# Deferred sums, evacuations, key transposes and exponentials, and one feed-forward split issued earlier, in a hybrid decoder layer

## Chip, cores and metric

The kernel runs on one core of one Trainium2 chip. The metric is the time of one execution on the device in microseconds (us); three runs are shown for the kernel before, and one further execution was taken with the hardware profiler.

## What is computed

One decoder layer over 512 tokens of width 1024, in float32. Three token mixers read the same normed input; their outputs are projected, gated, summed and projected again; a SwiGLU feed-forward follows. Both halves are residual.

```python
h = rms_norm(x, g_mix);  proj = h @ w_in             # q,k,v of two mixers, q of the third, three gates
y_m = moba_attention(rope(norm(q_m)), rope(norm(k_m)), v_m)    # 8 heads of 64; at 512 tokens: causal softmax
y_f = fox_attention(norm(q_f), norm(k_f), v_f, log_sigmoid(f_logit + b))   # 8 heads, cumulative bias
mk, mv = split(rms_norm(mem, g_mem) @ w_mem_kv)      # 256 memory tokens, 4 heads of 128
y_c = memory_attention(norm(q_c), norm(mk), mv)
merged = sum(sigmoid(a_i) * (y_i @ w_br_i)); x = x + merged @ w_out
h2 = rms_norm(x, g_ffn); x = x + (silu(h2 @ w_gate) * (h2 @ w_up)) @ w_down
```

## The kernel before

**Arithmetic.** Every float32 operand of a projection is split in two: a rounded high part, copied by ScalarE (`w_hi`, `hT` and so on), and the rest, a subtraction on VectorE (`w_lo`, the second half of `hT`). A product is then three passes on TensorE: high by high, high by low, low by high. Some products (units of the input projection, the gate and up matrices) are done with seven block products instead of eight, which needs sums of operand blocks first; `sums_of_h` makes those of the normed input: eight `whole_h` (one 128x512 addition each), eight `th_sum` (one 128x512 each) and four two-stage splits `th_split`.

**Order.** The order of instructions is written by hand. `mm` issues one matmul and counts estimated time; after each 1,250 ns of that (six matmuls of 512 columns, twelve of 256) it calls `tick` (L278). A tick (1) splits one weight piece ahead (`split_next`: the low part left over from the last tick, then the next high part), (2) runs what `later(n, fn)` has put off by n ticks (`run_due`), (3) takes steps from the list of work beside the matmuls (`side`, filled by `beside`, at a rate per tick), (4) runs what was left in `pend`. `flush_side` empties the list and then runs (2) and (4) twice more without a matmul. Each engine works through its own queue in this order, so an instruction that waits holds up those behind it on its engine.

**First stretch.** `mem_groups` projects the memory tokens, keys first, then values (48 matmuls, eight ticks, each). Beside it run the squares of x, and from the 11th tick on four steps of `turn_x`: each transposes two column blocks of the scaled x, and `evac_split` (L318) takes the bank out, high part on ScalarE, low part on VectorE. `rms_mem` makes the memory tokens' row norms. After `flush_side` come the values' evacuations (`vslots`), the sums of h, and the query projection `head_chunk(NT, 128, ...)`, 96 matmuls or 16 ticks, reading four weight pieces in turn, six matmuls each in the first row of tokens. The memory keys' `head_chunk(MT, 128, ..., lag=22)` has put off its own steps: norm factors on VectorE and ScalarE, a multiplication on POOL per 128 tokens (`norm`, L565), and one step per head at which the keys are transposed (`turn`, L622).

**Attention.** Four lists of 16 units each (two of `moba`, two of `fox`) run beside projections through `attention`: at step n the scores of unit n (L924), its masking and row minimum on VectorE (`softmax`, L935 to L945); the product with the values of a half two steps after its transposes; the transposes of unit n-4 (`turn`, L975, evacuated by `evac_split`); and last the exponential of unit n on ScalarE (`exps`, L953), which puts off by one tick the reciprocal (VectorE, L956) and the multiplication of the row (POOL, L957). The memory attention has a list of its own, which the diff leaves alone.

**Feed-forward start.** The second half of the output projection does four groups of 128 tokens. After the third, `turn2` and `right_split` prepare the first two right-hand operands. After the fourth, the last row norm is made, the put-off work is drained, ScalarE loads the table of silu, and `product` goes through the block products in the order of `FIRST`: (0, M1), (0, M2), (1, M1), (1, M2), ... `split_op(u, m)` (L1250) is the split of a left operand: high part on ScalarE (L1254), low part on VectorE (L1257). That of (1, M1) is issued from the first hooks of the first product.

Of the kernel before, what the change touches and what calls it, by code (L numbers as in the profile page):

```python
# [19 lines left out]
NT = S // P  # L20
M = 256
MT = M // P
D = 1024
KD = D // P
# [18 lines left out]
def hybrid_layer(ctx, tc, rope, x, mem, g_mix, w_in, b_forget, g_q_moba, g_k_moba, g_q_fox,  # L43
# [274 lines left out]
    def later(n, fn):  # L318
        deferred.append([n, fn])


    def evac_split(hi, lo, src, scale=None, late=False):
        if scale is None:
            act.activation(hi, src, AF.Copy)

            def low():
                dve.tensor_tensor(lo, src, f32(hi), op=OP.subtract)
        else:
            act.activation(hi, src, AF.Copy, scale=scale)

            def low():
                dve.scalar_tensor_tensor(lo, src, scale, f32(hi), op0=OP.mult, op1=OP.subtract)
        if late:
            pend.append(low)
        else:
            low()

    def rsqrt(ss, inv_n, w, delay=None, rows=None, nh=1, out=None):

# [90 lines left out]
    gcol = consts.tile([P, NG], F32, name="gcol")  # L430
# [120 lines left out]
    def head_rest(raws, tw, ss, ntok, d, kind, blocks, lag, rows=None, e=2, out=None):  # L551

        nh = tw // d
        w = ntok * nh
        if rows is not None:
            e = lag - 5
        rs = rsqrt(ss[:, :w], 1.0 / d, w, e, rows=rows, nh=nh, out=out)

        def of_tiles(t0, n):
            per = 1024 // tw  # L560
            return raws[t0 // per][:, t0 % per * tw:(t0 % per + n) * tw]

        def norm(t0, n):
            r3 = of_tiles(t0, n).rearrange("p (g d) -> p g d", d=d)
            pool.tensor_tensor(r3, r3, rs[:, t0 * nh:(t0 + n) * nh, None].to_broadcast([P, n * nh, d]),  # L565
                               op=OP.mult)

        def rotate():
            j = 0 if blocks[0][0] == GQM else 1
            r4 = of_tiles(0, ntok).rearrange("p (t h d) -> p t h d", t=ntok, h=nh)  # L570
            tmp = small.tile([P, ntok, nh, 16], F32, name="rtmp", tag="rtmp", bufs=1)
            for a in (0, 8):
                pool.tensor_tensor(
                    tmp[:, :, :, a:a + 8], r4[:, :, :, 8 - a:16 - a],
                    sg[:, j, :, None, a:a + 8].to_broadcast([P, ntok, nh, 8]), op=OP.mult)
            pool.tensor_tensor(r4[:, :, :, :16], r4[:, :, :, :16],
                               cg[:, j, :, None, :].to_broadcast([P, ntok, nh, 16]), op=OP.mult)
            pool.tensor_tensor(r4[:, :, :, :16], r4[:, :, :, :16], tmp, op=OP.add)

        n = 512 // tw  # L580
        for i in range(ntok // n if out is None else 0):
            later(e + 3 + i, lambda i=i: norm(i * n, n))
        if kind == "rope":
            later(e + 5, rotate)

        def turn_pair(blk):
            gc, dst, i, gains = blocks[blk]
            g = gains[:, gc:gc + 1]
            tb = bank("a")
            for tt in range(ntok):  # L590
                pe.transpose(tb[:, tt * P:(tt + 1) * P],  # L591
                             of_tiles(tt, 1)[:, blk * P:(blk + 1) * P], ident)
            if gc in (GQM, GQF):
                o = slot("qT", F32R)
                dst[i] = o
                o2 = [(o[:, 0:512], o[:, 0:512]), (o[:, 512:1024], o[:, 512:1024])]
            else:
                ks = [slot("kT", F32R), slot("kT", F32R)]
                dst[i] = ks
                o2 = [(k[:, 0:512], k[:, 512:1024]) for k in ks]  # L600
            for h, (hi, lo) in enumerate(o2):
                r = slice(64 * h, 64 * h + 64)
                act.activation(hi[r], tb[r], AF.Copy, scale=g[r])
            for h, (hi, lo) in enumerate(o2):
                r = slice(64 * h, 64 * h + 64)
                q = slice(64 - 64 * h, 128 - 64 * h)
                dve.scalar_tensor_tensor(lo[q if gc in (GQM, GQF) else r], tb[r], g[r],
                                         f32(hi[r]), op0=OP.mult, op1=OP.subtract)
            if gc not in (GQM, GQF):
                def double():  # L610
                    nc.gpsimd.dma_start(ks[0][64:128, :1024], ks[0][0:64, :1024])
                    nc.gpsimd.dma_start(ks[1][0:64, :1024], ks[1][64:128, :1024])
                later(1, double)

        def turn(blk):
            if d == 64:
                return turn_pair(blk)
            gc, dst, i, gains = blocks[blk]
            tb = bank("a")
            w = ntok * P  # L620
            for tt in range(ntok):
                pe.transpose(tb[:, tt * P:(tt + 1) * P],  # L622
                             of_tiles(tt, 1)[:, blk * P:(blk + 1) * P], ident)
            o = slot("qkT", F32R)
            evac_split(o[:, :w], o[:, w:2 * w], tb[:, :w], gains[:, gc:gc + 1])
            dst[i] = (o[:, :w], o[:, w:2 * w])
        order = sorted(range(len(blocks)), key=lambda blk: blocks[blk][2])
        for j, blk in enumerate(order):
            later(lag + (j if d == 128 or len(blocks) == 2 else 2 * j), lambda blk=blk: turn(blk))
# [23 lines left out]
        later(2, lambda: scale_x(2 * half))  # L653
        later(2, lambda: scale_x(2 * half + 1))

    def turn_x(k):
        tb = bank("a")
        for t in range(NT):
            pe.transpose(tb[:, t * P:(t + 1) * P], x_t[t][:, k * P:(k + 1) * P], ident)
        o = slot("hT", F32R)  # L660
        evac_split(o[:, :512], o[:, 512:1024], tb, gcol[:, GMIX + k:GMIX + k + 1])
        hT.append((o[:, :512], o[:, 512:1024]))


# [46 lines left out]
    def sums_of_h(first):  # L711
        for k in range(KD):
            later(first + k, lambda k=k: whole_h(k))
        n = first + KD
        for name in ("T1", "T2", "T3", "T4"):
            for j in range(2):
                later(n, lambda name=name, j=j: th_sum(name, j))
                n += 1
            for stage in range(2):
                later(n + stage, lambda name=name, stage=stage: th_split(  # L720
                    "N2" if name == "T2" else name, stage))
            n += 1
# [82 lines left out]
    def both(f, *args):  # L805
        return lambda: [f(*a) for a in args]

    def last_square(t):
# [3 lines left out]
    beside([idle, idle, small_gains, lambda: square_x(0), lambda: last_square(1),  # L812
            both(mem_square, (0, 0), (1, 0)), lambda: [square_x(2), last_square(3)], idle,
            both(mem_square, (0, 1), (1, 1)), idle]
           + [both(turn_x, (k,), (k + 1,)) for k in range(0, KD, 2)], 1.0)
    later(12, rms_mem)

    turn_mem(0, (split_next, split_next))
    pre = mem_groups(lambda: turn_mem(1))
    head_chunk(MT, 128, [(GKC, KC, h, gcol) for h in range(4)], lag=22, pre=pre, rows=rs_mem)  # L820
    vslots = [slot("memv", F32R) for _ in range(MT)]
    pre = mem_groups()
    flush_side()
    for t in range(MT):
        later(1 + t, lambda t=t, ps=pre[t]: evac_split(
            vslots[t][:, 0:512], vslots[t][:, 512:1024], ps, rs_mem[:, t:t + 1]))
    pre = None
    sums_of_h(1)
    pace["ahead"] = 3
    rs_q = consts.tile([P, NT * 4], F32, name="rs_q")  # L830
    nrs_q = consts.tile([P, NT * 4], F32, name="nrs_q")
    head_chunk(NT, 128, [(GQC, QC, h, gcol) for h in range(4)], lag=3, rs=rs_q)
    later(5, lambda: dve.tensor_scalar(nrs_q, rs_q, -1.0, None, op0=OP.mult))


# [80 lines left out]
    def attention(pairs, Q, K, V, Y, bias, sign=None):  # L916
# [89 lines left out]
        steps = []  # L1006
        for n in range(len(units) + LAG + 2):
            def step(n=n):
                if n < len(units):
                    scores(*units[n])  # L1010
                    softmax(*units[n])
                m = n - LAG - 2
                if 0 <= m < len(units) and units[m][2] % 2 == 1:
                    p, s, i = units[m]
                    values(p, s, i // 2)
                m += 2
                if 0 <= m < len(units):
                    turn(*units[m])
                if n < len(units):
                    exps(*units[n])  # L1020
            steps.append(step)
        return steps

# [345 lines left out]
    for t in range(NT):  # L1369
        if t == 2:  # L1370
            pace["ahead"] = 0
            load_quarters(1, ("S1", "S3", "A22"))
        out_group(t, 1, Ws)
        norm2(t)
        if t == 2:
            for kh, name in ((0, "B11"), (1, "B21")):
                turn2(kh, 0)
                right_split(name, Xf[kh, 0], 2)
    while deferred:
        run_due()  # L1380
        run_pend()
# [242 lines left out]
    at = {x: n for n, x in enumerate(order)}  # L1624
    todo = [[] for _ in range(len(order) + 1)]

    todo[0] += [lambda: split_op(1, "M1"), lambda: split_op(1, "M2")]
    todo[1] += [lambda: sums(1, "S2")]
    todo[2] += [lambda: turn2(1, 1), lambda: turn2(0, 1), lambda: right_split("B22", Xf[1, 1])]
    todo[3] += [lambda: sums(1, "S4"), lambda: right_sum("T1", Xf[0, 0], Xf[0, 1], OP.subtract),  # L1630
# [95 lines left out]
```

## Time and profile before

| | |
|---|---|
| three runs, us | 862.44, 863.42, 864.17 (median 863.42) |
| profiled execution, us | 863.53, of which the span from first to last instruction is 861.8 |
| TensorE matmul busy | 844.8 us, 98% of the span |
| VectorE, ScalarE, POOL busy | 660.6, 471.9, 221.6 us |
| mean granted TensorE clock | 0.998 of full speed |
| DMA | 126.10 MB, mean 146 GB/s |

A group of instructions is listed with its busy time and with the idle time of its engine just before it. Ends of matmuls are modelled: their starts are the firmer numbers.

### The profile page before, as it was taken

The page shows a single profiled execution, that of the slowest core. Times are in us where ns is not written, and L with a number is a line of the kernel's source. Part 1 is how long each engine was busy: PE and PEld are TensorE (multiplying, and loading weights), DVE is VectorE, ACT ScalarE, POOL GpSimd, SP SyncE. Part 2 cuts the span into 40 slices and gives each one's busy share as a digit, 9 for nine tenths or more (in the row PEclk, how much of TensorE's full clock was granted, in tenths as well). Part 3 has the DMA queues.
Part 4 walks back from the last instruction along what each step waited for, and adds up shares of the span by engine and source line. Part 5 has one row for each costly group of instructions (what it writes and reads, how often), then busy time and mean ns, then how long its engine had stood idle before and what let it go on. Part 6 is the DMA issues. An engine that isn't in the chain of part 4 may idle for free.

```text
span 861.8 us, 13979 instructions
## 1 busy us (share of the span) xinstructions
PE 844.8 (98%) x5204; PEld 755.3 (88%) x5204; DVE 660.6 (77%) x1135; ACT 471.9 (55%) x816; POOL 221.6 (26%) x306
## 2 busy tenths in 40 slices
PE   7889999999999999999999999999999999999998
PEld 5668999899878888988888888999999999988886
DVE  4887689779677576668655837898979898997985
ACT  5936656567765656656534525453334444474671
POOL 5110318221522553534310002333220222110220
PEclk9999999999999999999999999999999999999999
DMA  9922347326611460541692535999885989774992
GB/s 314 342 33 74 74 123 185 61 63 186 143 53 47 126 150 22 148 122 51 186 204 74 172 105 116 232 189 183 169 175 84 191 151 218 176 179 152 241 263 79
DMA packets 141283, 126.10 MB, mean 146 GB/s; under 512 B 5840, under 2 KB 120072, under 8 KB 141216
## 3 DMA queue, kind: packets, MB, share of 16 engines
q1 hardware_dynamic: 107840, 95.21, 37.8%
q0 software_dynamic: 32192, 27.89, 21.0%
q10 hardware_dynamic: 1184, 2.12, 0.8%
q8 instruction: 41, 0.67, 0.3%
q14 instruction: 26, 0.21, 0.1%
HBM read 116.79 MB, written 4.21 MB: 140 GB/s over the span
## 4 chain that ended last, share of the span: by engine, by line
PE 83%; DVE 8%; ACT 4%; DMA 2%; issue 1%; SPq 1%; POOL 0%; ACTq 0%; DVEq 0%; POOLq 0%
PE ps_m L302 39%; PE ps_a L1396 12%; PE ps_m L1396 9%; PE ps_a L1549 9%; PE ps_a L986 3%; PE ps_m L1549 3%; PE ps_a L302 2%; PE ps_a L924 2%; PE ps_a L975 2%; DMA x_t<-in_x_dram 2%; DVE w_lo L237 1%; DVE wl L1257 1%; ACT w_hi L234 1%; DMA w_raw<-in_w_in_dram 1%; PE ps_a L591 1%
## 5 line engine op out<-in xcount | busy, mean ns | idle before, releaser
L237 DVE TENSOR_TENSOR w_lo<-w_raw,w_hi 128x1024 fp32r<-128x1024 f32 (+2 forms) x88 | 108.1, 1240 | 31.1 <-ACT w_hi L234 30.5
L302 PE MATMUL ps_m<-w_hi,hT 128*128 128x256 f32 (+2 forms) x464 | 123.0, 339 | 0.0
L302 PE MATMUL ps_m<-hT,w_hi 128*128 128x512 f32 x384 | 121.3, 397 | 0.0
L1396 PE MATMUL ps_a<-xh,wl 128*128 128x256 f32 x352 | 100.0, 284 | 1.0 <-DVE wl L1257 0.8
L1396 PE MATMUL ps_a<-xh,wh 128*128 128x256 f32 x352 | 99.8, 283 | 0.2 <-ACT wh L1254 0.2
L1396 PE MATMUL ps_a<-xl,wh 128*128 128x256 f32 x352 | 99.6, 283 | 0.0
L234 ACT ACTIVATE w_hi<-w_raw 128x1024 fp32r<-128x1024 f32 (+2 forms) x88 | 86.4, 1003 | 2.7 <-issue 2.5
L302 PEld LDWEIGHTS ps_m<-w_hi,hT 128*128 128x128 f32 x464 | 80.8, 191 | 7.2
L302 PEld LDWEIGHTS ps_m<-hT,w_hi 128*128 128x128 f32 x384 | 69.5, 189 | 12.6
L302 PE MATMUL ps_m<-w_lo,hT 128*128 128x256 f32 (+2 forms) x232 | 76.7, 331 | 1.5 <-DVE w_lo L237 1.5
L1549 PE MATMUL ps_a<-dh,dr 128*128 128x512 f32 x242 | 76.6, 390 | 0.1
L302 PE MATMUL ps_m<-hT,w_lo 128*128 128x512 f32 x192 | 75.0, 391 | 0.0
L1396 PE MATMUL ps_m<-xh,wh 128*128 128x256 f32 x264 | 74.7, 283 | 0.0
L1396 PE MATMUL ps_m<-xh,wl 128*128 128x256 f32 x264 | 74.7, 283 | 0.0
L1396 PE MATMUL ps_m<-xl,wh 128*128 128x256 f32 x264 | 74.7, 283 | 0.0
L1439 ACT ACTIVATE z<-z 128x512 f32<-128x512 f32 x22 | 13.9, 632 | 105.3 <-DVE z L765 105.3
L1231 POOL DMA_DIRECT2D wq<-in_w_gate_dram x22 | 31.2, 1419 | 152.7 <-DMA wq<-in_w_gate_dram 69.7
L1396 PEld LDWEIGHTS ps_a<-xh,wl 128*128 128x128 f32 x352 | 67.5, 192 | 1.6 <-DVE wl L1257 1.6
L1257 DVE TENSOR_TENSOR wl<-wq,wh 128x1024 fp32r<-128x1024 f32 x55 | 66.9, 1218 | 1.8 <-ACT wh L1254 1.4
L1396 PEld LDWEIGHTS ps_a<-xh,wh 128*128 128x128 f32 x352 | 67.5, 192 | 0.4 <-ACT wh L1254 0.4
L1396 PEld LDWEIGHTS ps_a<-xl,wh 128*128 128x128 f32 x352 | 67.5, 192 | 0.0
L957 POOL TENSOR_SCALAR p_t<-p_t,rc 128x128 f32<-128x128 f32 (+1 forms) x64 | 39.0, 609 | 105.1 <-DVE rc L956 101.6
(281 smaller groups left out, 2204.7 us busy)
## 6 DMA issues: line engine op xcount, KB each, us to landing
w_raw<-in_w_in_dram SPq DMA_DIRECT2D x45, 512.0 KB, 4.3
wq<-in_w_gate_dram SPq DMA_DIRECT2D x55, 256.0 KB, 5.1
wq<-in_w_up_dram SPq DMA_DIRECT2D x55, 256.0 KB, 5.8
dq<-in_w_down_dram SPq DMA_DIRECT2D x25, 512.0 KB, 5.5
wq<-in_w_gate_dram POOLq DMA_DIRECT2D x22, 256.0 KB, 8.2
wq<-in_w_up_dram POOLq DMA_DIRECT2D x22, 256.0 KB, 10.1
dq<-in_w_down_dram POOLq DMA_DIRECT2D x10, 512.0 KB, 7.9
w_raw<-in_w_mem_kv_dram SPq DMA_DIRECT2D x8, 512.0 KB, 11.1
```

The costliest lines, as they stand in the source:

```text
L234: act.activation(hi[:, c], r[:, c], AF.Copy)
L237: dve.tensor_tensor(lo[:, c], r[:, c], f32(hi[:, c]), op=OP.subtract)
L302: pe.matmul(ps, lhsT, rhs, start=start, stop=stop)
L924: pe.matmul(ps[:, :n], Q[p][:, s * 512 + i * P:s * 512 + (i + 1) * P], K[p][s][:, b * 512:b * 512 + n], start=b == 0, stop=b == 1)
L957: pool.tensor_scalar(pt[:, :nk], pt[:, :nk], rc, 1.0, op0=OP.mult, op1=OP.mult)
L975: pe.transpose(tb[:, j * P:(j + 1) * P], pt[:, j * P:(j + 1) * P], ident)
L986: pe.matmul(yb[:, :256], V[p][:, j, 2 * s:2 * s + 2, :], PT[b][:, j, :], start=(j == 0 and b == 0), stop=(j == nj - 1 and b == 1))
L1231: e.dma_start(t[:, g * 512:(g + 1) * 512].rearrange("p (k c) -> p k c", k=4), dsrc(w, kh * 512 * DFF + f0 + fh * P, [[DFF, P], [P * DFF, 4 ...
L1257: dve.tensor_tensor(full(lo), full(r), f32(full(hi)), op=OP.subtract)
L1396: pe.matmul(ps[:, g * 256:(g + 1) * 256], w[a][:, g, k, :], r[b][:, k, :], start=n % 12 == 0, stop=n % 12 == 11)
L1439: act.activation(z[:, :, 0, :], z[:, :, 0, :], AF.Silu, scale=1.0 - 2 * j)
L1549: pe.matmul(acc_d[m][t2], r[a][:, e * 256 + t2 * P:e * 256 + (t2 + 1) * P], w[b][:, e * 512:(e + 1) * 512], start=(p == 0 and e == 0 and ( ...
```

## The change

Six places are touched; no arithmetic is added or taken away.

- `evac_split(late=...)` takes a number of ticks as well; `turn_x` passes one on, and the last pair of column blocks (6 and 7) has its two low parts put off by 3.
- `rms_mem` goes from 12 to 14 ticks.
- Memory keys: `lag` from 22 to 26, with the norm factors at `lag - 9` instead of `lag - 5`, so only the transposes move. Query heads: `lag` from 3 to 4.
- Values' evacuations: from 1 and 2 ticks to 5 and 6. `sums_of_h`: first step from 1 to 8, and with it all that follows in it.
- `attention`: the exponential of unit n-1 comes first in step n, where that of unit n came last in step n.
- The split of (1, M1): high part behind the right-hand operands after the third output group, low part with the drain (a delay of 50 ticks that is not reached before it).

```diff
-        if late:
+        if not late:
+            low()
+        elif late is True:
             pend.append(low)
         else:
-            low()
+            later(late, low)
@@ head_rest
-            e = lag - 5
+            e = lag - 9
@@ turn_x
-    def turn_x(k):
+    def turn_x(k, delay=None):
...
-        evac_split(o[:, :512], o[:, 512:1024], tb, gcol[:, GMIX + k:GMIX + k + 1])
+        evac_split(o[:, :512], o[:, 512:1024], tb, gcol[:, GMIX + k:GMIX + k + 1], late=delay)
@@
-           + [both(turn_x, (k,), (k + 1,)) for k in range(0, KD, 2)], 1.0)
-    later(12, rms_mem)
+           + [both(turn_x, (k,), (k + 1,)) for k in range(0, KD - 2, 2)]
+           + [both(turn_x, (KD - 2, 3), (KD - 1, 3))], 1.0)
+    later(14, rms_mem)
...
-    head_chunk(MT, 128, [(GKC, KC, h, gcol) for h in range(4)], lag=22, pre=pre, rows=rs_mem)
+    head_chunk(MT, 128, [(GKC, KC, h, gcol) for h in range(4)], lag=26, pre=pre, rows=rs_mem)
...
-        later(1 + t, lambda t=t, ps=pre[t]: evac_split(
+        later(5 + t, lambda t=t, ps=pre[t]: evac_split(
...
-    sums_of_h(1)
+    sums_of_h(8)
...
-    head_chunk(NT, 128, [(GQC, QC, h, gcol) for h in range(4)], lag=3, rs=rs_q)
+    head_chunk(NT, 128, [(GQC, QC, h, gcol) for h in range(4)], lag=4, rs=rs_q)
@@ attention, step(n)
+                if 0 < n <= len(units):
+                    exps(*units[n - 1])
                 if n < len(units):
                     scores(*units[n])
                     softmax(*units[n])
...
-                if n < len(units):
-                    exps(*units[n])
@@ output projection, after the third group
                 right_split(name, Xf[kh, 0], 2)
+            split_op(1, "M1", 50)
@@
-    todo[0] += [lambda: split_op(1, "M1"), lambda: split_op(1, "M2")]
+    todo[0] += [lambda: split_op(1, "M2")]
```

## Rows read from the trace of the kernel before

**Rows 1.** The page: busy time, share of the span, instructions of each engine.

```profile
PE 844.8 (98%) x5204; PEld 755.3 (88%) x5204; DVE 660.6 (77%) x1135; ACT 471.9 (55%) x816; POOL 221.6 (26%) x306
```

**Rows 2.** Waits of TensorE, whole span: us in total, times, longest.

```profile
PE ps_m L302 <- DVE w_lo L237: 2.5, 4, 1.0
...
PE ps_a L986 <- DVE y L994: 0.6, 1, 0.6
PE ps_a L975 <- POOL p_t L957: 0.4, 1, 0.4
PE ps_a L986 <- DVE pt L327: 0.3, 1, 0.3
```

**Rows 3.** Timeline of TensorE, query projection: start, duration, instruction, [idle before].

```profile
39.56 0.39 PE L302 MATMUL ps_m<-w_hi,hT 128*128 128x512 f32 x1
...
42.31 0.50 PE L302 MATMUL ps_m<-w_lo,hT 128*128 128x512 f32 x1 [1.00 <-DVE w_lo L237]
...
45.84 0.50 PE L302 MATMUL ps_m<-w_lo,hT 128*128 128x512 f32 x1 [0.52 <-DVE w_lo L237]
...
58.82 0.33 PE L622 MATMUL ps_a<-ident,raw 128*128 128x128 f32 x1 [1.12 <-POOL raw L565]
...
68.16 0.61 PE L302 MATMUL ps_m<-hT,w_hi 128*128 128x512 f32 x2
```

**Rows 4.** Chain that ended last, 55 to 75 us: start, us, piece.

```profile
59.15 2.20 PE ps_m L302 x6
...
61.77 1.97 PE ps_m L302 x6
63.74 0.22 PE ps_a L622 x2
63.95 1.40 PE ps_m L302 x6
...
65.57 5.47 PE ps_m L302 x24
```

**Rows 5.** One stretch: us, TensorE busy (instructions), granted clock, DMA share, GB/s.

```profile
59.50:60.00 0.50, 0.50 (x3) 0.50 0.00 0
```

**Rows 6.** Timeline of VectorE, query projection.

```profile
39.72 1.40 DVE L332 SCALAR_TENSOR_TENSOR hT<-ps_a,gcol,hT 128x512 fp32r<-128x512 f32 x2
41.04 2.35 DVE L237 TENSOR_TENSOR w_lo<-w_raw,w_hi 128x1024 fp32r<-128x1024 f32 x2
...
43.97 0.68 DVE L672 TENSOR_TENSOR xf<-hT 128x512 f32<-128x512 f32 x1
...
55.65 0.17 DVE L348 TENSOR_TENSOR rr<-rr,rsm 128x8 f32<-128x8 f32 x1
```

**Rows 7.** Timeline of POOL, key norms.

```profile
55.97 2.80 POOL L565 TENSOR_TENSOR raw<-raw,rr 128x512 f32<-128x512 f32 x2 [10.72 <-DVE rr L348]
```

**Rows 8.** Timeline of VectorE, start of the second attention list.

```profile
239.67 0.17 DVE L1118 TENSOR_TENSOR z<-ps_m,bfor 128x8 f32<-128x8 f32 x1 [1.03 <-ACT v L324]
```

**Rows 9.** Timeline of POOL, first and fourth attention lists.

```profile
164.95 1.54 POOL L957 TENSOR_SCALAR p_t<-p_t,rc 128x256 f32<-128x256 f32 x1 [1.71 <-DVE rc L956]
...
386.00 0.82 POOL L957 TENSOR_SCALAR p_t<-p_t,rc 128x128 f32<-128x128 f32 x2
```

**Rows 10.** Timeline of TensorE, first transposes of the fourth list.

```profile
386.41 0.33 PE L975 MATMUL ps_a<-ident,p_t 128*128 128x128 f32 x1
```

**Rows 11.** Timeline of all engines, start of the feed-forward.

```profile
529.05 0.63 ACT L1287 ACTIVATE sqh<-x 128x512 f32<-128x512 f32 x1 [1.44 <-DVE x L1286]
...
531.49 0.75 DVE L1315 TENSOR_SCALAR h<-x,rr 128x1024 f32<-128x1024 f32 x1 [0.27 <-DVE rr L364]
...
531.94 2.01 ACT L1254 ACTIVATE wh<-wq 128x1024 fp32r<-128x1024 f32 x2
...
533.03 2.36 DVE L1257 TENSOR_TENSOR wl<-wq,wh 128x1024 fp32r<-128x1024 f32 x2 [0.79 <-ACT wh L1254]
...
534.31 0.39 PE L1396 MATMUL ps_a<-xh,wl 128*128 128x256 f32 x1 [0.76 <-DVE wl L1257]
```

## The prediction, made before the changed kernel was seen

> **What bounds the kernel.** I read the page first. TensorE is busy for 98% of the span, the next engine for 77% [rows 1], so the time is TensorE's own work plus the moments at which it stands, and an edit is worth what it removes of those. The list of TensorE's waits shows where they are; the reader is to see how short it is: low parts of weights 2.5 us, in the attention 0.6 + 0.4 + 0.3 = 1.3 us, and nothing larger that the change can reach except the key norms [rows 2, 3]. Third, TensorE's timeline in the query projection. Twenty-four of its matmuls take 5.47 us, 0.228 each, and a pair of transposes 0.22 [rows 4]. So the 96 matmuls and four pairs of key transposes should take 96 x 0.228 + 4 x 0.22 = 22.8 us; from 39.56 to 68.16 they took 28.6 [rows 3]. This stretch loses 5.8 us, far more than its idle marks sum to, for two reasons. Idle is counted from modelled ends, and a matmul's modelled end is some 0.15 us behind the start of the next. And after the two waits for POOL, the longer 1.12 us, TensorE runs at half clock: 0.50 granted, which is 1.2 GHz [rows 3, 5]. The six matmuls after it take 2.20 us and the next six 1.97 where 1.40 is normal, so this alone costs 0.80 + 0.57, and 0.2 on the transposes between: some 1.6 us [rows 4]. Last, VectorE's and POOL's timelines show why TensorE stood.
>
> **Query projection: sums of h, evacuations, key transposes.** VectorE is late here. Between the low parts of the weights it does the values' evacuations and one `whole_h` per tick, 0.68 us each [rows 6]. The norm factors of the memory keys come out at 55.8 behind all this, POOL multiplies from 55.97 to 58.8, and the transposes wait [rows 6, 7]. Moved seven ticks on, the sums leave that place: from the 18th to the 23rd tick VectorE has only low parts, so the factors come when their tick does, and the transposes are put four ticks behind that as well (a tick is 1.4 us [rows 4]). I count the waits for POOL and the clock loss as gone.
>
> The waits for low parts go only in part. The two at 42.31 and 45.84 are for the 2nd and the 4th weight piece of the query projection [rows 3]. Before, VectorE does the last two `hT` low parts (1.40) and then the low parts of the 2nd and 3rd piece, until 43.39 [rows 6]. Now the two `hT` parts stand between those two: the 2nd piece comes some 1.3 us sooner, at about 40.7, before TensorE wants it (42.31 - 1.15 = 41.16; the 1.15 is the idle 1.00 and the 0.15 of modelled end). The 3rd still ends at 43.4 to 43.5, since the same work lies ahead of it plus two small instructions of `rms_mem`; TensorE, no longer held, wants it six matmuls on, at 41.16 + 1.37 = 42.5. So a wait of about 1.0 us stays, one piece later. The 4th ends one low part (half of 2.35, 1.18) behind, at 44.6, wanted at 44.9: no wait. I leave 1.15 with the refill and take 5.8 - 1.15 = **4.6 us**. Bounds: 5.8 if that wait goes too; 2.0 if the clock still falls (1.6) and another 1.0 us wait turns up.
>
> Costed at nothing: `rms_mem` two ticks on and the queries' transposes one tick on (the first query head's transposes still come five ticks ahead of the first memory scores); the values' evacuations (read only by the memory attention's products, after the query projection; the third query group, which wants their bank, begins four ticks after the first of them). With the cover gone, each costs one evacuation, 0.7 us (half of the 1.40 [rows 6]).
>
> The sums now lie beside the gates and the first memory scores. They are 16 additions of 0.68 and four low parts of 1.18, 15.6 us of VectorE [rows 6], all moved as one block; the last split is done at the 45th tick, and the first product that reads a sum starts at the 54th, so eight ticks cover it. Without that cover the price is the backlog, below as a rival.
>
> **Exponentials a step later.** Before, ScalarE's exponential of unit n waits for VectorE's row minimum of the same step, everything behind it on ScalarE waits too, and VectorE then waits for that: `z` stood 1.03 us for ScalarE's `v`, which was queued behind an exponential [rows 8]. With the exponential a step later its minimum is old, and neither engine holds the other. VectorE gets earlier, and what TensorE waited for in the second list (a bank taken out by `y`, a low part of `pt`, the first multiplied row) with it. Against this, the multiplied row is a step later while its transposes are not. In the fourth list the first multiplication starts at 386.00 and its transposes at 386.41 [rows 9, 10]: no room there. But POOL starts it late because an addition is queued ahead of it, and that stays; the reciprocal is now behind one more masking and is still ready before POOL is free. In the other three lists no multiplied row is as close to its transposes, and the one wait for such a row is 0.4 [rows 2]; what can be lost at a start is at most a step (six matmuls and a unit's own, 1.6 us). I take **1.2 us** of the 1.3 idle. Bounds: 1.8 with modelled ends, and -1.6 (a full step lost once).
>
> On this edit a rule can be weighed. A multiplication of 256 columns took 1.54 us when VectorE was doing a low part, where two smaller ones in a row take 0.82 [rows 9]. The Trainium skill, GPSIMD Engine Reference, section Key points, says that POOL shares its way to SBUF with VectorE and is slowed by VectorE instructions with two SBUF inputs; the trace agrees. By it a row that moves next to a low part is about 1.1 us later than I count, and the sum 5.5 instead of 6.6 if that hits one unit without room.
>
> **Feed-forward split.** ScalarE is idle for 1.44 us before 529.05, and one high part takes 1.0 [rows 11]: the (1, M1) copy fits and delays nothing. Without the gap it would push the last row norm by 1.0. Its low part starts when `h` is done, 531.49 + 0.75 = 532.24, instead of 533.03; at 1.18 each it ends at 533.4. TensorE started the matmul that needs it at 534.31 [rows 11]; it now can at 533.45: **0.86 us**. A short wait of some 0.4 stays. Bounds: 0, if the slot of the copy is freed late, and 1.3.
>
> **Sum.** 4.6 + 1.2 + 0.86 = 6.6 us. The profiled execution took 863.53, its span 861.8 and 1.7 around it; the runs' median is 863.42. 863.5 - 6.6 = 856.9; I say **857.0**.
>
> **Rivals.**
> *Late rows* (0.12): the exponentials give nothing or lose up to a step. For it: the room at 386.41 is nil. Against it: the addition ahead on POOL. Time: 863.5 - 4.6 - 0.9 = 858.0, to 859.7 with a step lost.
> *The early stretch keeps its loss* (0.10): the clock falls all the same, or the wait that stays is twice as long. For it: TensorE still stands 1.0 us at 42.5, after earlier stops. Against it: at 42.31, with the same wait, the clock did not fall; it fell only after two waits for POOL. Time: 863.5 - 2.0 - 1.2 - 0.9 = 859.4, to 860.8 with a second such wait.
> *Given back* (0.08): VectorE's block of 15.6 us hits the low parts of the gate pieces, which stand behind it in its queue. For it: the block now has such work behind it. Against: pieces are split three ahead there, and VectorE is busy for only 77% on average. If TensorE waits for half the block, 863.5 - 6.6 + 7.8 = 864.7; a third to a half gives 862.1 to 864.7, and I count the case as no change.
> *Slower* (0.06): multiplied rows come late at the starts of the second and fourth list, each by a full step (1.6) and a slowed multiplication (1.54 against half of 0.82: 1.1 [rows 9]), and the clock falls after each (1.6): 4.3 twice, against 4.6 + 0.9 gained: 866.6. It decides from a stop as long as that before 58.82, if the reciprocal slips behind POOL's addition and TensorE has no other work between.
>
> The forecast has 0.64: 855.4 to 858.4 by itself. The range is to leave out the cases without change and slower (0.14) and little more: 855.2 to 861.0. A measurement of this kernel tells 0.2% (1.7 us) from no change. Faster 0.86, same 0.08, slower 0.06.
>
> **What would show it.** TensorE: no wait for POOL at L622, granted clock 1.00 from 55 to 65, one wait of about 1 us for a low part near 42.5, 39.56 to the end of the query projection in 24 us. VectorE: `xf` rows after 50. Attention: TensorE's waits at L975 and L986 below 0.4 in sum, and no new ones in the first, third and fourth list. Feed-forward: the `wh` of (1, M1) before the table load, a wait of about 0.4 for its `wl`. The prediction is wrong if TensorE waits for low parts between 65 and 100 us, if new waits for POOL's `p_t` appear, or if the half-clock stretch turns up elsewhere.

## The result and the profile after

The changed kernel takes 858.24 us (median of five, 858.01 to 858.80), the kernel before, run beside it, 862.44 (861.23 to 864.17): a ratio of 0.995, interval 0.9935 to 0.9964, 4.2 us less. The profiled execution took 858.01 us, its span 856.2. Lines have moved: the key transposes are L624, the memory attention's scores, transposes and products L850, L885 and L896, the attention's transposes and products L979 and L990, its multiplied row L961, the feed-forward's products L1401.

The page of the changed kernel, busy time as in [rows 1], and TensorE's waits as in [rows 2]:

```profile
PE 841.0 (98%) x5204; PEld 753.7 (88%) x5204; DVE 657.9 (77%) x1135; ACT 469.9 (55%) x816; POOL 224.7 (26%) x306
```

```profile
PE ps_m L302 <- DVE w_lo L237: 2.0, 3, 1.1
...
PE ps_a L302 <- DVE mempl L327: 0.9, 1, 0.9
PE ps_a L979 <- POOL p_t L961: 0.5, 1, 0.5
PE ps_a L885 <- DVE yT L327: 0.5, 1, 0.5
PE ps_a L990 <- DVE pt L327: 0.2, 1, 0.2
```

The waits for POOL's `raw`, for `y` and for `wl` are gone from the list (a rest of the last shows below, in the starts). Four are new, 2.1 us together: `mempl` and `yT` in the memory attention, a multiplied row (`p_t`) in the fourth attention list, and a low part of `pt` in the third; the `p_t` and `pt` of [rows 2] were in the second list and are gone. Busy time hardly tells anything of this; the list of waits does.

To see where the time went, take the same TensorE instruction in both timelines and subtract. The table, called the ledger from here on, says how far ahead the changed kernel is, and what each stretch adds to that:

| TensorE instruction | before, us | after, us | ahead | stretch adds |
|---|---|---|---|---|
| first query product | 39.56 | 39.12 | 0.44 | |
| first memory scores | 82.30 | 77.39 | 4.91 | +4.47 |
| transposes after the memory attention's second head | 112.67 | 109.56 | 3.11 | -1.80 |
| projection in the second list | 265.79 | 260.09 | 5.70 | +2.59 |
| projection behind the third list | 364.36 | 359.46 | 4.90 | -0.80 |
| late output projection | 515.02 | 510.20 | 4.82 | -0.08 |
| feed-forward, 600 us | 600.09 | 594.14 | 5.95 | +1.13 |

The 0.44 at the start cannot be put down to the change: other profiles with nothing changed up to there were between 0.37 behind and 0.95 ahead. The change gives 5.51 us, 4.5 + 1.7 + 1.1 less 1.8. That the two profiled executions differ by just as much (863.53 - 858.01 = 5.52) is because the 0.44 is lost again at the end: from the start of the last matmul to the end of the span there were 4.19 us before and 4.63 after. Five of the fourteen profiles have the longer end; what it is was not followed. The largest entry that the prediction lacks is the -1.80.

TensorE's timeline in the query projection [rows 3] and in the memory attention:

```profile
39.12 0.39 PE L302 MATMUL ps_m<-w_hi,hT 128*128 128x512 f32 x1
...
43.28 0.50 PE L302 MATMUL ps_m<-w_lo,hT 128*128 128x512 f32 x1 [1.06 <-DVE w_lo L237]
...
62.63 0.71 PE L302 MATMUL ps_m<-hT,w_hi 128*128 128x512 f32 x2
...
101.95 0.38 PE L302 MATMUL ps_a<-w_hi,xh 128*128 128x256 f32 x1 [0.89 <-DVE mempl L327]
...
104.83 0.63 PE L885 MATMUL ps_a<-ident,p_t 128*128 128x128 f32 x4 [0.47 <-DVE yT L327]
```

VectorE in the same places, the first part as in [rows 6]:

```profile
40.70 1.40 DVE L332 SCALAR_TENSOR_TENSOR hT<-ps_a,gcol,hT 128x512 fp32r<-128x512 f32 x2
42.02 5.75 DVE L237 TENSOR_TENSOR w_lo<-w_raw,w_hi 128x1024 fp32r<-128x1024 f32 x5
...
50.39 0.68 DVE L675 TENSOR_TENSOR xf<-hT 128x512 f32<-128x512 f32 x1
...
51.60 0.17 DVE L350 TENSOR_TENSOR rr<-rr,rsm 128x8 f32<-128x8 f32 x1
...
82.00 0.68 DVE L858 TENSOR_REDUCE mn<-ps_a 128x2 f32<-128x512 f32 x1
...
82.79 1.22 DVE L237 TENSOR_TENSOR w_lo<-w_raw,w_hi 128x1024 fp32r<-128x1024 f32 x1
84.21 0.17 DVE L871 RECIPROCAL rc<-se 128x2 f32<-128x2 f32 x1 [0.19 <-ACT p_t L867]
85.16 1.33 DVE L702 TENSOR_TENSOR xl<-xt,xh 128x1024 fp32r<-128x1024 f32 x1 [0.78 <-ACT xh L698]
86.41 0.68 DVE L858 TENSOR_REDUCE mn<-ps_a 128x2 f32<-128x512 f32 x1
...
88.62 0.17 DVE L871 RECIPROCAL rc<-se 128x2 f32<-128x2 f32 x1 [1.33 <-ACT p_t L867]
88.70 0.67 DVE L858 TENSOR_REDUCE mn<-ps_a 128x2 f32<-128x512 f32 x1
```

The key norms' factors are ready at 51.8 instead of 55.8, earlier as forecast. But look at 82 to 87. The memory attention's units go round a loop on two engines: row minimum on VectorE, exponential on ScalarE, reciprocal on VectorE, and behind it in the queue the next minimum, 2.3 to 2.6 us a turn, with VectorE idle for 1.33 of it. Between the first minimum and the second now stands `xl`, the low part of the last of the four splits of the sums. It waits 0.78 for its high part, which stands on ScalarE behind the exponential:

```profile
82.97 0.57 ACT L867 ACTIVATE p_t<-ps_a,mn,nrs_q 128x256 f32<-128x256 f32 x1 [2.11 <-DVE mn L859]
...
84.07 1.05 ACT L698 ACTIVATE xh<-xt 128x1024 fp32r<-128x1024 f32 x1
```

So the second minimum comes at 86.41, 2.2 us after the reciprocal that frees it, though its scores were on TensorE from 80.85 on. In the kernel before, the loop had time to spare: its second and third minimum waited for TensorE's scores.

```profile
86.67 0.69 DVE L854 TENSOR_REDUCE mn<-ps_a 128x2 f32<-128x512 f32 x1 [0.44 <-PE ps_a L846]
...
90.13 0.69 DVE L854 TENSOR_REDUCE mn<-ps_a 128x2 f32<-128x512 f32 x1 [1.08 <-PE ps_a L846]
```

Now TensorE is 4.9 us sooner and that time is gone. The reading, before the experiments: this one split puts the loop behind, and TensorE meets it 15 us later as waits for `mempl` and `yT`, with which VectorE takes banks out.

The feed-forward's start, by ScalarE, VectorE and TensorE, against [rows 11]:

```profile
522.70 1.05 ACT L1258 ACTIVATE wh<-wq 128x1024 fp32r<-128x1024 f32 x1
...
527.10 2.35 DVE L1261 TENSOR_TENSOR wl<-wq,wh 128x1024 fp32r<-128x1024 f32 x2
...
528.04 0.28 PE L1401 MATMUL ps_a<-xl,wh 128*128 128x256 f32 x1
528.37 0.39 PE L1401 MATMUL ps_a<-xh,wl 128*128 128x256 f32 x1
```

The low part starts when `h` is done. The matmul that wants it starts 0.33 behind the one ahead of it, where 0.12 is usual: 0.2 us is left of the wait.

### The profile page after: what moved, and what is told of

Same layout as the page of the kernel before. It is cut to its first block, busy times and chain, and to the rows that moved or that the text cites. A ratio compares the mean times of both kernels' runs of the same rounds, so it can differ in the third digit from the quotient of the medians.

```text
span 856.2 us, 14049 instructions
## 1 busy us (share of the span) xinstructions
PE 841.0 (98%) x5204; PEld 753.7 (88%) x5204; DVE 657.9 (77%) x1135; ACT 469.9 (55%) x816; POOL 224.7 (26%) x306
## 4 chain that ended last, share of the span: by engine, by line
PE 80%; DVE 9%; ACT 6%; DMA 2%; issue 1%; POOL 0%; ACTq 0%; SPq 0%; DVEq 0%
PE ps_m L302 37%; PE ps_a L1401 12%; PE ps_m L1401 9%; PE ps_a L1554 9%; PE ps_m L1554 3%; PE ps_a L990 3%; PE ps_a L928 2%; PE ps_a L302 2%; PE ps_a L979 2%; DMA x_t<-in_x_dram 2%; DVE w_lo L237 1%; ACT w_hi L234 1%; DVE wl L1261 1%; PE ps_a L593 1%; ACT p_t L867 1%
## 5 line engine op out<-in xcount | busy, mean ns | idle before, releaser
L302 PE MATMUL ps_m<-w_hi,hT 128*128 128x256 f32 (+2 forms) x464 | 121.0, 336 | 0.0
L1401 PE MATMUL ps_a<-xh,wl 128*128 128x256 f32 x352 | 100.0, 284 | 0.3
L1401 PE MATMUL ps_a<-xh,wh 128*128 128x256 f32 x352 | 99.7, 283 | 0.0
L1401 PE MATMUL ps_a<-xl,wh 128*128 128x256 f32 x352 | 99.6, 283 | 0.0
L1401 PE MATMUL ps_m<-xh,wl 128*128 128x256 f32 x264 | 74.7, 283 | 0.0
L1401 PE MATMUL ps_m<-xh,wh 128*128 128x256 f32 x264 | 74.7, 283 | 0.0
L1401 PE MATMUL ps_m<-xl,wh 128*128 128x256 f32 x264 | 74.7, 283 | 0.0
L961 POOL TENSOR_SCALAR p_t<-p_t,rc 128x128 f32<-128x128 f32 (+1 forms) x64 | 40.4, 632 | 108.4 <-DVE rc L960 77.1
L1401 PEld LDWEIGHTS ps_a<-xh,wl 128*128 128x128 f32 x352 | 67.5, 192 | 0.9 <-DVE wl L1261 0.9
L1401 PEld LDWEIGHTS ps_a<-xh,wh 128*128 128x128 f32 x352 | 67.6, 192 | 0.0
L1401 PEld LDWEIGHTS ps_a<-xl,wh 128*128 128x128 f32 x352 | 67.5, 192 | 0.0
```

What stands on the lines that cost most here:

```text
L302: pe.matmul(ps, lhsT, rhs, start=start, stop=stop)
L961: pool.tensor_scalar(pt[:, :nk], pt[:, :nk], rc, 1.0, op0=OP.mult, op1=OP.mult)
L1401: pe.matmul(ps[:, g * 256:(g + 1) * 256], w[a][:, g, k, :], r[b][:, k, :], start=n % 12 == 0, stop=n % 12 == 11)
```

## Experiments

Each kernel ran against the kernel before on the same chip. What each stretch adds to the lead of TensorE over the profiled execution of before, in us, stretches as in the table above:

| kernel | query | memory attention | lists 1, 2 | list 3 | list 4 on | feed-forward | median, us |
|---|---|---|---|---|---|---|---|
| changed | +4.47 | -1.80 | +2.59 | -0.80 | -0.08 | +1.13 | 858.24 |
| early edits alone | +4.48 | -1.76 | +0.03 | +0.01 | -0.02 | 0.00 | 860.64 |
| exponentials alone | -0.04 | 0.00 | +2.59 | -0.78 | -0.08 | +0.01 | 860.44 |
| split alone | +1.60 | 0.00 | 0.00 | +0.02 | -0.03 | +1.12 | 861.49 |
| transposes alone | +3.73 | -0.01 | +0.02 | +0.02 | -0.02 | -0.02 | 860.22 |
| sums alone | +4.24 | -1.31 | +0.03 | +0.01 | -0.02 | -0.01 | 860.84 |
| changed, last split late | +4.46 | 0.00 | +2.02 | -0.78 | -0.11 | +1.11 | 857.41 |
| changed, sums at 5 | +4.56 | -0.01 | +2.60 | -0.80 | -0.08 | +1.10 | 856.36 |
| changed, sums at 3 | +4.44 | -0.01 | +2.60 | -0.77 | -0.09 | +1.15 | 856.52 |
| changed, sums at 1 | +4.12 | -0.01 | +2.60 | -0.78 | -0.08 | +1.13 | 856.34 |
| sums at 5, row sooner | +4.47 | -0.01 | +2.53 | -0.90 | +0.38 | +1.11 | 856.05 |
| before, second profile | +1.61 | 0.00 | +0.02 | +0.02 | -0.02 | +0.01 | 861.92 (one) |
| before, third profile | -0.04 | 0.00 | +0.02 | +0.01 | -0.02 | +0.03 | 862.98 (one) |

The stretches add up: the three groups of edits alone give the entries of the whole, to 0.05 us, but for one (split alone, +1.60 in a stretch that it does not touch), for which the last two kernels of the table were run.

**The three groups, each alone in the kernel before.** Early edits: all but the exponentials and the split. The other two:

```diff
+                if 0 < n <= len(units):
+                    exps(*units[n - 1])
...
-                if n < len(units):
-                    exps(*units[n])
```

```diff
+            split_op(1, "M1", 50)
...
-    todo[0] += [lambda: split_op(1, "M1"), lambda: split_op(1, "M2")]
+    todo[0] += [lambda: split_op(1, "M2")]
```

> The kernel before with the early group alone (low parts of hT, row norm of the memory tokens, key and query transposes, values' evacuations, sums of h); exponentials and feed-forward split as before. Theory (the sums of h, put off by seven ticks, make VectorE late at the memory attention's first row minimum): the query projection gains 4.6 us and 1.9 us of it are lost between 99 and 105 us, so about 2.7 us faster than before, with new waits of TensorE for low parts of mempl (0.9) and yT (0.5). Rival (these two waits come from the other edits): 4.6 us faster and no such waits.

> The kernel before with the exponentials a step later and nothing else. Theory from the ledger of the two traces: the waits of the second list go (2.5 us of lead gained there), the third and fourth lists lose 0.9 us, together about 1.7 us faster, and a wait of 0.5 us for POOL's row appears in the fourth list. Rival (the ledger of the lists owes part to the earlier edits): 1.2 us or less, as predicted, and no wait in the fourth list.

> The kernel before with the split of (1, M1) issued earlier and nothing else. Theory from the ledger: TensorE's waits for wh (0.15) and wl (0.76) both go, 1.1 us faster. As predicted: 0.86 us, with a wait of 0.4 for wl left. Either way under what the totals tell apart by much; the trace around 533 us decides.

Early: 860.64 against 862.24, ratio 0.9979 (0.997 to 0.9987). Both waits are there (0.85 and 0.46), so they are of this group. It is 1.6 us faster rather than the 2.7 of the ledger, for the reason found with the last two runs. Exponentials: 860.44, ratio 0.998 (0.9971 to 0.9988), 1.73 in the ledger, with the wait of 0.51 for POOL's row in the fourth list; the theory, not the 1.2. Split: 861.49, ratio 0.9991 (0.9983 to 1.0), which the totals hardly tell from no change; 1.12 in the ledger.

**Are the sums what the memory attention waits for?** In the changed kernel, the sums put off less, in three steps:

```diff
-    sums_of_h(8)
+    sums_of_h(5)
```

> The changed kernel with the sums of h put off to the 5th tick instead of the 8th (before: 1st). Theory (they hold up VectorE at the memory attention): first row minimum of the memory attention about 2 to 3 us nearer behind its scores than 3.9 us, the waits for mempl and yT at 102 and 105 us gone, 1.9 us faster than the changed kernel: about 856.3. Rival one (the memory attention's own chain of minimum, exponential, reciprocal is slower than TensorE's steps): the waits stay, 858.2. Rival two (the sums are again among the urgent low parts): waits for POOL or low parts come back in the query projection, 859 to 861.

> The changed kernel with the sums of h at the 3rd tick. Theory: as at the 5th, no wait in the memory attention and one wait for a low part in the query projection, 856.4; if whole_h comes between urgent low parts, 0.5 more. Rival (each tick earlier costs the low parts): 857 and over.

> The changed kernel with the sums of h where they were before (1st tick). Theory (with the transposes four ticks later the sums need not move for the key norms, only for the low parts): no wait for POOL, no half clock, the second wait for a low part (0.5) back in the query projection, none in the memory attention: lead at the memory attention's end about 4.3 instead of 3.1, so about 857.0, between the changed kernel and the one with the 5th tick. Rival (moving the sums is what frees the key norms): waits for POOL back, 858.5 or more.

At the 5th, 3rd and 1st tick the medians are 856.36 (ratio 0.9932, 0.9918 to 0.9945), 856.52 (0.9928, 0.9916 to 0.9941) and 856.34 (0.9927, 0.9913 to 0.994), 1.7 to 1.9 us under the changed kernel (the kernel before had 862.24, 862.61 and 862.61 beside them, 862.44 beside the changed one). None of them waits in the memory attention. Rival one is out: the loop by itself keeps up with TensorE arriving 4 to 5 us sooner. One detail was expected wrongly: the first minimum is only 0.9 us sooner with the sums at 5 (81.12); it is the second that moves, from 86.41 to 83.42, and each later minimum up to 100.41 is some 2.7 us sooner as well. With the sums back at the 1st tick the key norms are as late as before (POOL works from 56.19 to 58.98) and still nobody waits: the transposes come at 61.6. The second wait for a low part was expected back and is not.

**The load, or the one split?** Sums at 8, and only the last split ten ticks on; its result is first read by the last product of its unit:

```diff
-                later(n + stage, lambda name=name, stage=stage: th_split(
+                later(n + stage + 10 * (name == "T4"), lambda name=name, stage=stage: th_split(
```

> The changed kernel with one of the four splits of the sums (T4, the last; ScalarE's xh and VectorE's xl) put off by ten more ticks; the sums stay at the 8th tick. Theory (not the load of VectorE but this one split between the first and the second row minimum, whose high part stands behind an exponential, holds up the memory attention): second row minimum at about 83.5 instead of 86.4, no waits for mempl and yT, 1.9 us faster than the changed kernel, 856.3. Rival (15.6 us of VectorE's work are too much there, wherever they stand): the waits stay or come a few us later, 857.5 to 858.5.

VectorE's timeline of this kernel:

```profile
81.95 0.69 DVE L858 TENSOR_REDUCE mn<-ps_a 128x2 f32<-128x512 f32 x1
...
82.75 1.23 DVE L237 TENSOR_TENSOR w_lo<-w_raw,w_hi 128x1024 fp32r<-128x1024 f32 x1
84.17 0.17 DVE L871 RECIPROCAL rc<-se 128x2 f32<-128x2 f32 x1 [0.18 <-ACT p_t L867]
84.25 0.67 DVE L858 TENSOR_REDUCE mn<-ps_a 128x2 f32<-128x512 f32 x1
```

The first minimum and all ahead of it are where they were (81.95, 82.00 in the changed kernel); only the split is gone from between, and the second minimum follows at 84.25, 2.2 us sooner. The memory attention loses 0.00. So it is the one instruction pair in that place and not the block of 15.6 us. The total is 857.41 (ratio 0.9945, 0.9933 to 0.9958) and not 856.3: TensorE waits 0.4 for an accumulation of VectorE at 152.94, where VectorE is 0.7 us later than with the sums at 5. By the same instructions in both timelines VectorE is 0.8 us later from 84 on, 1.8 behind the moved split (107.29), 1.2 at 116.49 and 0.7 from 145 to 152: it has too little idle time there to make it up. That is read from the traces; no run tests it.

**Sums or transposes: which one frees TensorE from POOL?** Each alone, in the kernel before:

```diff
-            e = lag - 5
+            e = lag - 9
...
-    head_chunk(MT, 128, [(GKC, KC, h, gcol) for h in range(4)], lag=22, pre=pre, rows=rs_mem)
+    head_chunk(MT, 128, [(GKC, KC, h, gcol) for h in range(4)], lag=26, pre=pre, rows=rs_mem)
...
-    head_chunk(NT, 128, [(GQC, QC, h, gcol) for h in range(4)], lag=3, rs=rs_q)
+    head_chunk(NT, 128, [(GQC, QC, h, gcol) for h in range(4)], lag=4, rs=rs_q)
```

```diff
-    sums_of_h(1)
+    sums_of_h(8)
```

> The kernel before with the transposes of keys (four ticks) and queries (one tick) later and nothing else of the change; the sums stay where they were. Theory (the two waits for POOL, 0.54 and 1.12, bring the half clock): POOL ends at 58.8 as before, the first key transposes come at about 61, both waits go and the clock stays at 1.00 from 55 to 65, the two waits for low parts (1.00, 0.52) stay: 1.7 + 1.6 = 3.3 us faster, nothing lost in the memory attention, 858.9. Rival (the clock falls for the earlier stops too): 1.7 us faster, 860.6, with 0.50 granted somewhere before 62.

> The kernel before with the sums of h put off from the 1st to the 8th tick and nothing else. Theory: the norm factors of the keys come some 4 us earlier, POOL ends before 55, both waits for POOL and the half clock go without the transposes being moved, 3.3 to 4.6 us gained in the query projection; 1.9 us of it lost in the memory attention: 859.5 to 860.8. Rival (the transposes at the 29th tick are too early even so): a wait for POOL of 0.5 or more stays and the gain is under 2.5 us before the loss: 861.5 or more.

Either does. Transposes alone: 860.22, ratio 0.9977 (0.9969 to 0.9986); POOL is done at 59.14, the first transposes start at 62.45, clock 1.00 from 55 to 65, 3.73 us in the ledger and nothing lost. Sums alone: 860.84, ratio 0.9983 (0.9974 to 0.9993); 4.24 gained, and 1.31 given back, with waits of 0.40 and 0.46 for `mempl` and `yT`. The early group holds both and has no more of it than 4.48.

**The late row.** Sums at 5, and the reciprocal and the multiplication at the end of the step of the late exponential:

```diff
-            later(1, scale)
+            pend.append(scale)
```

> The changed kernel with the sums of h at the 5th tick, and with reciprocal and row multiplication of an attention unit at the end of the step of its (late) exponential instead of a tick on, so that POOL has the row as early as in the kernel before. Theory (the row a step late costs 0.5 in the fourth list, behind POOL's addition, and some 0.8 of lead at the ends of the second and third lists): the wait for p_t in the fourth list goes and 0.5 to 1.3 us are gained on 856.4: 855.1 to 855.9. Rival (VectorE's reciprocal now waits for ScalarE's exponential, and what is behind it too): the waits of the second list for y and pt come back, 857 to 858.

What it is to mend, POOL's and TensorE's timelines of the changed kernel at the start of the fourth list, against [rows 9, 10]:

```profile
379.81 1.29 POOL L1082 TENSOR_TENSOR acc<-acc,th 128x512 f32<-128x512 f32 x1 [1.22 <-DVE th L1080]
381.10 0.36 POOL L961 TENSOR_SCALAR p_t<-p_t,rc 128x128 f32<-128x128 f32 x1
381.44 1.28 POOL L1082 TENSOR_TENSOR acc<-acc,th 128x512 f32<-128x512 f32 x1
382.71 1.45 POOL L961 TENSOR_SCALAR p_t<-p_t,rc 128x256 f32<-128x256 f32 x1
...
384.21 0.44 PE L979 MATMUL ps_a<-ident,p_t 128*128 128x128 f32 x2 [0.51 <-POOL p_t L961]
```

Before, the first two multiplications (128 and 256 columns, 0.36 and 0.47 us) ran in a row; now an addition of 1.28 comes between them, and the second takes 1.45. In the new kernel they run in a row again:

```profile
380.10 0.82 POOL L961 TENSOR_SCALAR p_t<-p_t,rc 128x128 f32<-128x128 f32 x2
380.89 1.29 POOL L1082 TENSOR_TENSOR acc<-acc,th 128x512 f32<-128x512 f32 x1
```

The wait is gone and the fourth list adds +0.38 instead of -0.08. The second and third lists do not recover, so their losses (0.3 and 0.5, at the last products with values, 277 and 360 in the kernel before) are not the row's lateness. The timelines name another cause. ScalarE's in the kernel before, then ScalarE's, VectorE's and TensorE's in the changed kernel, at the second of the two places:

```profile
356.85 0.23 ACT L359 ACTIVATE ry<-ra 128x32 f32<-128x32 f32 x1
356.99 0.47 ACT L324 ACTIVATE pt<-ps_a 128x384 fp32r<-128x384 f32 x1
```

```profile
351.51 0.71 ACT L957 ACTIVATE p_t<-p_t,mn 128x512 f32<-128x512 f32 x1
...
352.22 0.47 ACT L324 ACTIVATE pt<-ps_a 128x384 fp32r<-128x384 f32 x1
...
352.79 0.56 DVE L327 TENSOR_TENSOR pt<-ps_a,pt 128x384 fp32r<-128x384 f32 x1 [1.00 <-ACT pt L324]
...
354.47 0.69 DVE L327 TENSOR_TENSOR pt<-ps_a,pt 128x512 fp32r<-128x512 f32 x1
...
354.72 0.28 PE L990 MATMUL ps_a<-pt,v 128*128 128x256 f32 x1
355.21 1.10 PE L990 MATMUL ps_a<-pt,v 128*128 128x256 f32 x7 [0.22 <-DVE pt L327]
```

The last exponential of the list, a step later, now stands on ScalarE ahead of the copy of `pt`. VectorE's low parts come later by it, and TensorE's second product starts 0.49 us behind the first, where 0.12 is usual. At the first place it is the same (exponential at 267.12, copy at 267.84, products 0.34 apart). This is read from the traces; no run moves the last exponential alone. The median, 856.05 (ratio 0.993, 0.9918 to 0.9942), is the lowest of all, but 0.3 under 856.36 is not told apart here.

**The clock in the kernel before.** Two more profiles of the unchanged kernel:

> The kernel before, unchanged, profiled once more. Theory (the half clock after the two waits for POOL comes in some executions and not in others: it was there in the profile of before and with the exponentials alone, not with the split alone, though the waits of 0.5 to 0.6 and 1.1 us were the same in all three): the waits are there again, and the time is about 863.5 if 0.50 is granted between 59 and 63 us and about 861.9 if the clock stays at 1.00. Rival (the fall follows the waits every time): 0.50 granted and about 863.5.

> The kernel before, unchanged, a further time. The same two theories: 863.5 with the half clock between 59 and 63 us, 861.9 without it; one execution at 1.00 with both waits there is enough against the rival.

TensorE's timeline and a stretch of half a microsecond, the second profile first, then the third. Behind the stretch's length stand the busy time (and instructions) of TensorE, its weight loads, VectorE, ScalarE and POOL, then the granted clock, DMA share and GB/s:

```profile
57.39 0.33 PE L622 MATMUL ps_a<-ident,raw 128*128 128x128 f32 x1 [0.58 <-POOL raw L565]
58.83 0.33 PE L622 MATMUL ps_a<-ident,raw 128*128 128x128 f32 x1 [1.12 <-POOL raw L565]
```

```profile
59.50:60.00 0.50, 0.50 (x4) 0.41 (x3) 0.29 (x1) 0.17 (x1) 0.00 (x0) 1.00 0.00 0
```

```profile
56.90 0.33 PE L622 MATMUL ps_a<-ident,raw 128*128 128x128 f32 x1 [0.58 <-POOL raw L565]
58.34 0.44 PE L622 MATMUL ps_a<-ident,raw 128*128 128x128 f32 x1 [1.12 <-POOL raw L565]
```

```profile
59.50:60.00 0.50, 0.50 (x3) 0.40 (x2) 0.50 (x2) 0.00 (x0) 0.00 (x0) 0.50 0.00 0
```

The same waits, and once 1.00 of the clock (2.4 GHz), once 0.50 (1.2 GHz). Of the five profiles with these waits, the half clock is in three (before, its third profile, exponentials alone) and not in two (its second profile, split alone). It costs 1.6 us each time, the +1.60 and +1.61 of the table. The rival is out. The mean granted clock of the other executions says how often it comes; it is 0.997 or 0.998 in the three profiles with the half clock, 0.999 in the two without. Of 59 of the kernel before that ran beside the experiments, 18 have 0.998 or less, with a median of 863.5 us, and 41 have 0.999 or 1.00, with 862.0. With the exponentials alone it is 3 of 11, with the split alone 5 of 11, and in the kernels without the two waits none of 64. So the half clock was seen only with these waits, and in about three of ten executions. The times: 861.92 as expected, and 862.98, 0.5 under the 863.5 expected, for a start 0.55 us sooner.

## Why the prediction came out as it did

*Right: what bounds it.* All that moved the time are waits of TensorE and the clock behind two of them. VectorE's busy time fell by 2.7 us and ScalarE's by 2.0 with no instruction taken away, and that says nothing about the total.

*Right in size, wrong in what it is compared with: the query projection.* 4.6 forecast, 4.47 measured. One wait stays, one piece later: 1.06 at 43.28. No wait for POOL, clock 1.00 from 39 to 63. But 1.6 of it is the half clock, which only some executions of before have; against one without it the gain is 2.9. The sum was made against a profiled execution that had it, 863.53, and the text set that equal to the median of three. The five executions beside the changed kernel have 862.44. So the gain against the profile is 5.5, by medians 4.2, and against the executions of before at full clock (862.0) 3.8. The forecast of the time takes no harm from this, since none of the changed kernel's five executions shows the half clock; the gain of 6.6 does.

*Right effect, two causes given for one: the stall for POOL.* The text put the sums' move first and the transposes "as well". Either is enough; with the sums left at the 1st tick the query projection keeps 4.12 of 4.47. So moving the sums to the 8th tick gained some 0.35 us there and cost 1.8 later.

*The step that failed: "all moved as one block; the last split is done at the 45th tick, and the first product that reads a sum starts at the 54th, so eight ticks cover it."* That asks who reads the moved work. It does not ask what is queued behind it on VectorE: the memory attention's row minima, from the 42nd tick on. The cover was priced at the 54th tick, and its price, the rival *Given back*, was put at the gate pieces' low parts between 65 and 100 us, where no wait appeared. The place was the memory attention, and the price 1.8 us, for one split in a loop that had no slack left once TensorE came sooner.

*Too small: exponentials.* 1.2 forecast, 1.7 measured, inside the bounds. The three waits of the second list went, and with them 2.59 us of lead where 1.3 was idle. Not forecast: 0.8 lost at the ends of the second and third lists, where the place of the exponential, now ahead of the copy of `pt` on ScalarE, had not been weighed, and the wait of 0.51 for `p_t` in the fourth, the rival *Late rows* in small. By the text's own signs it is wrong here: a new wait for `p_t` appears, and TensorE's waits in the attention, L979 and L990 now, come to 0.7 and not below 0.4. The first row there, with "no room", came in time; the second did not, behind the addition. It also ran beside a low part, 1.45 us where 0.47 is usual for 256 columns. (The 0.82 of [rows 9] joins a row of 128 and one of 256 columns; the slowing of 1.1 that the text takes from it holds all the same, 1.54 - 0.47.) The Trainium skill, GPSIMD Engine Reference, Key points, says that POOL shares its SBUF interfaces with VectorE and contends there with VectorE instructions that have two SBUF inputs, as a low part has; this trace agrees. The low part beside it was slow too:

```profile
381.95 1.85 DVE L237 TENSOR_TENSOR w_lo<-w_raw,w_hi 128x1024 fp32r<-128x1024 f32 x1
```

It took 1.85 us where 1.22 is usual. But for its first 0.77 us it ran beside POOL's addition; low parts beside a slowed multiplication alone kept their time (1.23 us at 165.00 in the kernel before, 1.22 at 384.18 in the kernel with the sums at 5 and the row sooner). So its loss goes with the addition, as far as the traces show; no run separates the two.

*Too small by a rest: feed-forward split.* 0.86 forecast with 0.4 of a wait left; 1.13 measured with 0.2 left. TensorE's wait of 0.15 for the high part, just ahead of the one for the low part, went as well, and had not been counted.

Summed: 4.47 + 1.71 + 1.13 = 7.3 where 6.6 was forecast, less 1.80 in the memory attention. That the measured 858.24 is only 1.2 us above the 857.0 said is in part luck: two terms were too small by 0.8 together, which hides nearly half of the term that was missing.

## What to carry to other kernels

A block moved on an engine's queue costs nothing only if everything queued behind it has slack, not just its own readers: look for loops over two engines (minimum, exponential, reciprocal) at the place where it lands, since here one instruction that waits inside such a loop delayed every later turn. Where two edits remove the same stall, try each alone: here four ticks on the transposes did it without the sums. And a loss that a profile shows, above all one of the clock, should be looked for in a second profile before it is counted as a gain.

## What was not expected of the hardware

After the same two stops of TensorE (0.5 to 0.6 and 1.12 us) the granted clock fell to 0.50 in three profiles of five. It fell at about 59.5, 58.4 and 59.0 us, that is 0.6, 0.1 and 1.1 us behind the end of the second stop: not at a fixed distance from it. The Trainium skill, TensorE: Matmul & The Clock Gate, Part 1 (The HAM clock gate), says of the start of a kernel that what watches the activity runs freely, and that the same kernel differs from run to run; these five profiles show such a difference in the middle of one.
